# adaLN pieces of the second block in groups of four, all during the first block, in a two-block transformer on one core

## The chip, the core and the metric

The kernel runs on one core of one Trainium2 chip. The metric is the device time of one execution in microseconds (us), from the program's first to its last instruction; less is better. Inputs and weights lie in HBM, 582.56 MB of them are read once.

## The reference

256 latent tokens and 256 context tokens of width 1024, all in float32. A first block (adaLN, a mixer of bidirectional retention and mLSTM, a SwiGLU feed-forward) changes the latents; a second block of two layers follows. Each layer of the second block takes six vectors for shift, scale and gate from its own condition, once for the latents and once for the context:

```python
x = first_block(x, c, ctx, c_ctx, w_ada, ...)        # mixer, then x + g2 * swiglu(...)
for layer in range(2):                               # second block
    m_lat = split((silu(c_2) @ mod_w[layer] + mod_b[layer])[:, None, :], 6)
    m_ctx = split((silu(c_ctx_2) @ mod_w[layer] + mod_b[layer])[:, None, :], 6)
    h_lat = rms_norm(x_lat, norm1_g[layer]) * (1 + m_lat[1]) + m_lat[0]   # and h_ctx
    y = even_mixer(...) if layer == 0 else odd_mixer(...)   # window attention + gating; MLA + short conv
    x_lat = x_lat + m_lat[2] * y_lat
    h_lat = rms_norm(x_lat, norm2_g[layer]) * (1 + m_lat[4]) + m_lat[3]
    x_lat = x_lat + m_lat[5] * expert_choice_ffn(h_lat, ...)   # 16 experts, 32 tokens each
    # layer 0 does the same for the context
return rms_norm(x_lat, final_g)
```

`mod_w[layer]` is 1024 x 6144. It depends on the conditions alone, so these products can be made at any time before their layer.

## The kernel before

**The weight stream.** All weights come as pieces of up to 16 KB a partition (2 MB) in one order, written out with `seq(...)` (L220 to L227, L243). `Ring` (L48) puts the next piece of that order into whichever slot has just been used: `ring.done(slot)` issues its DMA on SP's queue (L69). Three slots, R0, R1 and R2, serve the dense stages; the expert stages have further ones (F, G, H, L, Y and others). A piece's slot is thus decided by which piece is used up first.

**The products.** `prod` (L331) splits a quarter of a piece at a time into a high and a low part (ACT at L303, then DVE at L304, into `w4k` or `w4p`) and makes three passes of 128x128 by 128x256 matmuls. Each job calls `tick()`, which takes one step of every generator in `beside`; `aside(...)` puts work there. In fin and fout, a piece `fin{i}` is 96 such matmuls, a pair of `fout` pieces 132.

**The adaLN pieces.** `moda0` to `moda11` are layer 0's, `modb0` to `modb11` layer 1's, 512 columns each. `mod_steps` (L354) is the generator of one: eight matmuls of 32 columns (`sT2`, the two conditions and zeros) against 512, four row groups side by side, into one of two `aux` PSUM banks; an evacuation to `ev`; four small matmuls with `selm` that turn `ev` into columns; an addition of the bias into MOD20 or MOD21. The profile counts two matmuls for each of these. In its rows the eight are `aux<-R,sT`, the four `aux<-cp,ev`.

**Stages in order.** Block 1's mixer ends with the product `wout`. A norm follows, then `fin0` to `fin10` and `fout0` to `fout7` (block 1's feed-forward), the even mixer (pieces `evkv`, `evin`, `evout`), the experts of layer 0, the odd mixer (`odq`, `odg`, ...) and the experts of layer 1. A scheduler decides each engine's order from the program.

**Where the pieces run before.** moda0 and moda1 after wout, moda2 and moda3 in fin, moda4 to moda6 in fout, moda7 to moda9 in the even mixer's attention, moda10, moda11 and modb0 to modb3 at its end, modb4 to modb11 in the odd mixer (`mods1`).

Of the kernel before, what the change touches and what calls it, by code (L numbers as in the profile page):

```python
# [14 lines left out]
P = 128  # L15
# [6 lines left out]
# pieces that come in parts, for the products that wait for them  # L22
# [6 lines left out]
class Rows:  # L29
    """An expert's piece with its four rows in more than one tile."""  # L30
# [17 lines left out]
class Ring:  # L48
    """Weight pieces in stream order through slots of 16 KB a partition."""
# [42 lines left out]
def body(ctx, tc, T, dbg=None, stop_at=None):  # L92
# [68 lines left out]
    # work in steps beside the products: each of their jobs takes a step of every generator  # L161
# [41 lines left out]
    # ---------------------------------------------------------------- weight stream  # L203
# [5 lines left out]
    def seq(*names):  # L209
# [12 lines left out]
        "wout0", "wout1", "moda0", "moda1")  # L222
# [20 lines left out]
    seq("odq0", "odg0", "modb4", "modb5", "odkv0", "oduq0", "odukv0",  "odg1", "modb6", "odg2", "modb7", "modb8",  # L243
        "modb9", "odout0", "odout1", "modb10", "modb11")
# [3 lines left out]
    # ---------------------------------------------------------------- constants and small loads  # L248
# [27 lines left out]
    selm = cp[:, 640:642]  # L276
    iota32 = cp[:, 642:674]
# [13 lines left out]
    # ---------------------------------------------------------------- shared parts  # L291
# [9 lines left out]
    def split(src, hi, lo):  # L301
        """src = hi + lo: hi keeps the bits of one pass, lo the rest."""
# [13 lines left out]
    def col(out, j, x, start=False):  # L316
        """A job of prod: 128 columns of the weights, from j * 128, as the partitions of out."""
# [6 lines left out]
    def tok(out, x, start=False):  # L324
        """A job of prod: tokens as the partitions of out, the weights' columns along it."""
# [5 lines left out]
    def prod(segments, jobs, quiet=False):  # L331
        """Each job's product over the rows of the weights' segments [128, k, n]; start: the first in its bank."""
# [21 lines left out]
    def mod_steps(name, sT, bias, MOD):  # L354
        """512 columns of both rows of silu(c) @ w + b, as columns of MOD[:, chunk, row], in steps."""
# [11 lines left out]
        ev = t2k() if name in ("modb10", "modb11") else work("ev", 512, 1)  # L367
# [3 lines left out]
        for c in range(4):  # L371
            mm(p2[:, 2 * c:2 * c + 2], ev[:, c * 128:c * 128 + 128], selm)
        dve.tensor_tensor(MOD[:, i * 4:i * 4 + 4, :], p2[:, :8].rearrange("p (c r) -> p c r", c=4),
                          bias[:, i * 4:i * 4 + 4, None].to_broadcast([P, 4, 2]), op=OP.add)

    def mod_steps0(name, sT, bias, MOD):
        """The same for the latents' row alone: weighted rows added up elementwise, then over the partitions."""
# [29 lines left out]
    def rstd_cols(ps, n, dim, half=False):  # L407
        """Columns [128, n] of 1 / sqrt(sum / dim + eps), halved if asked for, from sums."""
# [13 lines left out]
    def rms_bcast(chunks, ntok, dim):  # L422
        """1 / rms over the partitions and chunks of K-major [128, ntok] pieces, on every partition."""
# [11 lines left out]
    def norm_apply(X, rb, A, sh, hi, lo=None):  # L435
        """X * rstd * A + sh, K-major, 256 tokens: split into hi and lo, or whole in hi."""
# [38 lines left out]
    def sums_wide(bank):  # L475
        """The same with the tensor engine's sums, through a bank."""
# [33 lines left out]
    def rope(raw, sw, cosv, sinv, out, n, heads):  # L510
        """out = raw * cos + swap(raw) * sin; raw [128, heads * n] in SBUF."""
# [14 lines left out]
    # ================================================================ block 1  # L526
# [3 lines left out]
    sT2 = silu_c("cc2", cst.tile([P, KC * 32], F32, name="sT2"))  # L530
# [7 lines left out]
    def over_rms(X, read, U):  # L538
        """X / rms in U, before the scale and the shift are known."""
# [40 lines left out]
    # the first product starts with half of its rows  # L580
# [19 lines left out]
    # log of the decays, the same on every partition: columns (direction, head)  # L600
# [18 lines left out]
    # gates as rows: directions at partitions 0 and 32, the forget gates 64 further on  # L619
# [53 lines left out]
    # decays of the context's keys to its end (forward) and to its start (backward)  # L673
# [9 lines left out]
    # ---- projections  # L683
# [13 lines left out]
    def rope_pair(ps, scale, out):  # L697
        """Rotated heads of 128, two a bank: [128, 2, 256]."""
# [57 lines left out]
    def proj_T(name, post):  # L756
        """K-major [128, 256] products of the 512 columns, two a bank."""
# [16 lines left out]
    # ---- mLSTM and retention over the latent tokens  # L774
# [97 lines left out]
    def head_rstd(x, tag, dim):  # L872
        """Half of the rstd over each head's 128 of token-major [128, 512]."""
# [21 lines left out]
    # sigmoid(x) = (1 + tanh(x / 2)) / 2; the halves go into the factors beside it  # L895
# [1109 lines left out]
```

## Time and profile before

| | |
|---|---|
| median of three runs | 1931.47 us (1931.06 to 1933.48) |
| profiled execution, first to last instruction | 1936.9 us |
| mean granted TensorE clock | 0.939 |
| PE busy | 88% |
| weights and inputs read | 579.58 MB, 300 GB/s over the span |

The profile is of one execution, whose own time is its span. Where a view names an engine: PE is the tensor engine, DVE the vector engine, ACT the scalar engine, SP the engine whose queue issues nearly all DMAs. `R<-w_fin` is a DMA of a `fin` piece into a slot R.

### The profile page before, as it was taken

To read this page: it belongs to the slowest core of one execution; us is meant where nothing else is said; L and a number is where in the kernel's file an instruction comes from. 1 tells how busy PE (TensorE), PEld (TensorE's weight loads), DVE (VectorE), ACT (ScalarE), POOL (GpSimd) and SP (SyncE) were. 2 spreads that over 40 slices of the span, in tenths; PEclk is the share of its full clock that TensorE was granted. 3 is DMA by queue.
4 is the path that set the end of the run, shared out by engine and by line. 5 is a ranking of instruction groups with operands and counts; after the bars stand their busy time and mean duration, and the time that the engine had idled before them with its cause. 6 is when DMAs were issued, how large, how long until landed. Compare 5 with 4: busy or idle time off the path is not lost.

```text
span 1936.9 us, 29903 instructions
## 1 busy us (share of the span) xinstructions
PE 1696.5 (88%) x13020; PEld 1181.5 (61%) x13020; DVE 748.9 (39%) x1457; ACT 535.7 (28%) x927; POOL 52.1 (3%) x51
## 2 busy tenths in 40 slices
PE   7999999999999999799999989899999666575665
PEld 3999997989997678734433423368776323242333
DVE  4856785545566555502212102165653111010111
ACT  3323553445455543311010100043442100010000
POOL 0100020000001000000000000001000000000000
PEclk8999999999999999899999999999998988797877
DMA  9455456555633235699999999952687999999996
GB/s 354 183 199 218 158 192 228 195 226 182 251 129 111 113 141 216 261 408 425 428 428 427 427 428 427 423 207 109 239 326 306 425 426 426 425 425 426 426 427 261
DMA packets 53986, 582.56 MB, mean 301 GB/s; under 512 B 5984, under 2 KB 5984, under 8 KB 20576
## 3 DMA queue, kind: packets, MB, share of 16 engines
q1 hardware_dynamic: 53136, 577.90, 73.5%
q10 hardware_dynamic: 720, 2.75, 0.4%
q8 instruction: 102, 1.67, 0.3%
q14 instruction: 28, 0.23, 0.0%
HBM read 579.58 MB, written 1.05 MB: 300 GB/s over the span
## 4 chain that ended last, share of the span: by engine, by line
PE 56%; DMA 29%; issue 9%; DVE 4%; ACT 1%; POOL 0%; SPq 0%; DVEq 0%; ACTq 0%; POOLq 0%
PE acc L187 39%; PE aux L187 10%; DMA R<-w 8%; PE tr L187 5%; DMA H<-w 4%; DMA w4k<-w 3%; DMA F<-w 3%; DMA XC<-w 3%; DMA G<-w 2%; DMA L<-w 2%; PE tr L190 2%; DMA Y<-w 2%; PE lg L187 1%; DMA R<-w_in 1%; DMA cp<-cperm 1%
## 5 line engine op out<-in xcount | busy, mean ns | idle before, releaser
L187 PE MATMUL acc<-L,w4k 128*128 128x256 f32 (+3 forms) x1904 | 289.9, 343 | 17.1 <-DMA L<-w 14.0
L187 PE MATMUL acc<-H,w4k 128*128 128x256 f32 (+2 forms) x1608 | 245.8, 336 | 14.9 <-DMA H<-w 12.1
L187 PEld LDWEIGHTS acc<-L,w4k 128*128 128x128 f32 (+2 forms) x1904 | 218.5, 177 | 63.5 <-issue 33.1
L304 DVE TENSOR_TENSOR w4k<-R,w4k 128x1024 fp32r<-128x1024 f32 (+3 forms) x152 | 178.8, 1178 | 138.7 <-ACT w4k L303 137.1
L187 PEld LDWEIGHTS acc<-H,w4k 128*128 128x128 f32 (+2 forms) x1608 | 189.2, 176 | 54.6 <-issue 29.4
L303 ACT ACTIVATE w4k<-R 128x1024 fp32r<-128x1024 f32 (+3 forms) x152 | 154.3, 1017 | 223.1 <-PE acc L187 192.1
L187 PE MATMUL acc<-R,w4k 128*32 128x256 f32 (+1 forms) x1104 | 161.3, 549 | 58.2 <-DMA R<-w 58.2
L187 PEld LDWEIGHTS acc<-R,w4k 128*32 128x32 f32 (+1 forms) x1104 | 55.9, 139 | 147.5 <-DMA R<-w 71.7
L199 DVE COPY t2k<-acc 128x512 f32<-128x512 f32 x24 | 16.6, 691 | 283.3 <-PE acc L187 283.3
L187 PE MATMUL acc<-F,w4k 128*32 128x256 f32 (+2 forms) x624 | 89.1, 470 | 22.3 <-DMA F<-w 22.3
L197 ACT ACTIVATE w4p<-aux 32x512 f32<-32x512 f32 (+1 forms) x58 | 28.1, 485 | 256.3 <-PE aux L187 195.5
L187 PE MATMUL aux<-R,t2k 128*32 128x256 f32 (+2 forms) x592 | 84.2, 528 | 14.3 <-DMA R<-w 14.3
L199 DVE COPY w4p<-aux 32x512 f32<-32x512 f32 (+1 forms) x58 | 32.5, 560 | 144.4 <-ACT w4p L197 107.0
L187 PEld LDWEIGHTS acc<-F,w4k 128*32 128x32 f32 (+2 forms) x624 | 44.0, 144 | 56.3 <-DMA F<-w 26.7
L190 PEld LDWEIGHTS tr<-cp,t2k 128*128 128x128 f32 (+1 forms) x290 | 32.8, 146 | 72.9 <-ACT t2k L197 25.7
L197 ACT ACTIVATE t2k<-acc 128x512 f32<-128x512 f32 x24 | 14.3, 597 | 223.3 <-PE acc L187 223.3
L187 PE MATMUL acc<-G,w4k 128*128 128x256 f32 (+1 forms) x462 | 70.3, 333 | 6.2 <-DMA G<-w 6.2
L190 PE MATMUL tr<-cp,t2k 128*128 128x128 f32 (+1 forms) x290 | 47.6, 292 | 30.7 <-ACT t2k L197 12.1
L304 DVE TENSOR_TENSOR w4p<-R,w4p 128x1024 fp32r<-128x1024 f32 x43 | 53.1, 1235 | 41.2 <-ACT w4p L303 41.1
L187 PEld LDWEIGHTS aux<-R,t2k 128*32 128x32 f32 (+1 forms) x592 | 31.0, 138 | 59.3 <-issue 35.3
L187 PE MATMUL acc<-L,w4p 128*128 128x256 f32 x416 | 65.9, 281 | 0.0
L1265 DVE TENSOR_TENSOR t2k<-t2k,tr 128x256 f32<-128x256 f32 x16 | 6.7, 421 | 149.0 <-ACT t2k L1264 149.0
(465 smaller groups left out, 2635.6 us busy)
## 6 DMA issues: line engine op xcount, KB each, us to landing
R<-w SPq DMA_DIRECT2D x67, 2048.0 KB, 27.8
F<-w SPq DMA_DIRECT2D x23, 2048.0 KB, 29.4
H<-w SPq DMA_DIRECT2D x23, 2048.0 KB, 29.3
L<-w SPq DMA_DIRECT2D x23, 2048.0 KB, 26.2
Y<-w SPq DMA_DIRECT2D x23, 2048.0 KB, 28.5
R<-mod SPq DMA_DIRECT2D x22, 2048.0 KB, 8.8
R<-w_in SPq DMA_DIRECT2D x11, 2048.0 KB, 7.7
R<-w_fin SPq DMA_DIRECT2D x10, 2048.0 KB, 7.8
```

The source lines that it names most:

```text
L187: return pe.matmul(out, lhsT, rhs, start=start, stop=stop, **kw)
L190: return pe.transpose(out, in_, ident[:in_.shape[0], :in_.shape[0]])
L197: act.activation(out, in_, AF.Copy, scale=1.0 if scale is None else scale)
L199: dve.tensor_copy(out, in_)
L303: act.activation(rnd(hi), src, AF.Copy)
L304: dve.tensor_tensor(rnd(lo), src, hi, op=OP.subtract)
L1265: dve.tensor_tensor(hT[:, :256], sg[:, :256], pt[:, 256:], op=OP.mult)
```

## The change

The pieces run in groups of four. A group's four products go into one PSUM bank, each with a stationary shifted by two columns, so that they come to stand in rows of their own; one evacuation, four matmuls with an eight-column `selm` and one addition serve all four. All six groups are put beside the work after wout, as one chain. The stream alternates fin and mod pieces, then fout and mod pieces, and has no mod piece after evkv0. `need(name)` steps the chain until a piece has been issued. The comments and docstrings that the change also takes out are not shown.

```diff
+        "wout0", "moda0", "wout1", "moda1", "moda2")
+    mods = [f"moda{i}" for i in range(12)] + [f"modb{i}" for i in range(12)]
     for i in range(11):
-        seq(f"fin{i}", *{4: ['moda2'], 5: ['moda3']}.get(i, []))
-    seq("fout0", "fout1", "moda4", "fout2", "fout3", "moda5", "fout4", "fout5", "moda6", "fout6", "fout7")
-    seq("evkv0", "evin0", "evin1", "evin2", "moda7", "moda8", "moda9", "evout0", "evout1", "moda10", "moda11",
-        *[f"modb{i}" for i in range(4)])
+        seq(f"fin{i}", mods[3 + i])
+    for i in range(8):
+        seq(f"fout{i}", mods[14 + i])
+    seq("evkv0", *mods[22:], "evin0", "evin1", "evin2", "evout0", "evout1")
...
-    seq("odq0", "odg0", "modb4", "modb5", "odkv0", "oduq0", "odukv0",  "odg1", "modb6", "odg2", "modb7", "modb8",
-        "modb9", "odout0", "odout1", "modb10", "modb11")
+    seq("odq0", "odg0", "odkv0", "oduq0", "odukv0", "odg1", "odg2", "odout0", "odout1")
...
+    def mod_group(names, bias, MOD):
+        i0 = 4 * int(names[0][4:])
+        ps = None
+        for j, name in enumerate(names):
+            while not ring.has(name):
+                yield
+            s_, W = ring.get(name)
+            Wv = kv3(W)
+            ps = aux() if ps is None else ps
+            for k in range(2):
+                for q in range(4):
+                    mm(ps[32 * q:32 * q + 32, :], sT2[:, 2 * q + k, 6 - 2 * j:38 - 2 * j], Wv[:, 2 * q + k, :],
+                       start=j == 0 and k == 0, stop=j == 3 and k == 1, tile_position=(0, 32 * q), skip_group_check=True)
+            ring.done(s_)
+            yield
+        ev = work("ev", 512, 1)
+        evac(ev, ps)
+        yield
+        p2 = aux()
+        for c in range(4):
+            mm(p2[:, 8 * c:8 * c + 8], ev[:, c * 128:c * 128 + 128], selm)
+        dve.tensor_tensor(MOD[:, i0:i0 + 16, :].rearrange("p (i c) r -> p i c r", c=4),
...
+    def need(name):
+        while not ring.has(name):
+            tick()
+        return ring.get(name)
...
-    sT2 = silu_c("cc2", cst.tile([P, KC * 32], F32, name="sT2"))
+    sT2 = cst.tile([P, KC * 38], F32, name="sT2")
+    dve.memset(sT2, 0.0)
+    sT2 = sT2.rearrange("p (k m) -> p k m", k=KC)
+    act.activation(sT2[:, :, 6:8], S("cc2").rearrange("p (k m) -> p k m", k=KC), AF.Silu)
...
-    pre_ = aside(*[mod_steps(f"moda{i}", sT2, S("mod_b0"), MOD20) for i in [0, 1]])
+    groups_ = groups(*range(6))
...
-        s_, W = ring.get(f"fin{i}")
+        s_, W = need(f"fin{i}")
...
-        sa, Wa = ring.get(f"fout{2 * n4}")
-        sb, Wb = ring.get(f"fout{2 * n4 + 1}")
+        sa, Wa = need(f"fout{2 * n4}")
+        sb, Wb = need(f"fout{2 * n4 + 1}")
...
-    drain(mods_)
-    aside(*[mod_steps(f"moda{i}", sT2, S("mod_b0"), MOD20) for i in range(10, 12)],
-          *[mod_steps(f"modb{i}", sT2, S("mod_b1"), MOD21) for i in range(4)])
+    drain(groups_)
```

Every other `aside(mod_steps(...))` of moda and modb goes as well, and `mods1`.

**The boundary from wout to fin, on PE.** `acc<-H,w4p` is the end of wout, `tr<-ones` the norm's sums, `acc<-L,w4k` the first products of fin0. Before:

```order
L187 MATMUL acc_3324<-H_2829,w4p_3354 128x256
L187 MATMUL tr_3395<-ones,ss_3135 128x1
L187 MATMUL tr_3395<-ones,t2k_3383 128x1 x2
L187 MATMUL tr_3395<-ones,ss_3135 128x1
L187 MATMUL tr_3395<-ones,t2k_3383 128x1 x2
L187 MATMUL aux_3496<-cp,ev_3482 128x2 x4
L187 MATMUL aux_3502<-R_9_3131,sT_112 32x512 x8
L187 MATMUL tr_3406<-cp,rs_r_3404 128x128 x2
L187 MATMUL aux_3531<-cp,ev_3513 128x2 x4
```

Now:

```order
L187 MATMUL acc_3326<-H_2831,w4p_3356 128x256
L187 MATMUL aux_3450<-R_9_3133,sT_112 32x512
L187 MATMUL tr_3392<-ones,ss_3137 128x1
L187 MATMUL aux_3450<-R_9_3133,sT_112 32x512 x6
L187 MATMUL aux_3450<-R_10_3387,sT_112 32x512 x8
L187 MATMUL tr_3392<-ones,t2k_3385 128x1 x2
L187 MATMUL tr_3392<-ones,ss_3137 128x1
L187 MATMUL tr_3392<-ones,t2k_3385 128x1 x2
L187 MATMUL tr_3403<-cp,rs_r_3401 128x128 x2
L187 MATMUL acc_3464<-L_3391,w4k_3466 128x256
L187 MATMUL acc_3465<-L_3391,w4k_3466 128x256
L187 MATMUL aux_3450<-R_10_3490,sT_112 32x512 x8
```

moda1 (slot R_9) and moda2 (R_10) now stand among the norm's sums, where before the turn of moda0, moda1 and two more small turns stood behind them; no turn is there any more.

**The same place on SP's queue.** A cut piece comes in four DMAs (x4). Before, from wout1 on:

```order
L69 DMA R1_9_2848<-w_out 128x1024 x4
L69 DMA R2_9_3129<-mod0 128x4096
L69 DMA R0_9_3131<-mod0 128x4096
L69 DMA R2_10_3480<-w_fin 128x4096
L69 DMA R1_10_3385<-w_fin 128x1024 x4
L69 DMA R0_10_3511<-w_fin 128x4096
L69 DMA R1_11_3617<-w_fin 128x4096
```

Now, from moda0 on:

```order
L69 DMA R1_9_2850<-mod0 128x4096
L69 DMA R2_9_3128<-w_out 128x1024 x4
L69 DMA R0_9_3133<-mod0 128x4096
L69 DMA R1_10_3459<-w_fin 128x1024 x4
L69 DMA R2_10_3387<-mod0 128x4096
L69 DMA R0_10_3490<-mod0 128x4096
L69 DMA R2_11_3512<-w_fin 128x4096
```

fin0 (the cut `w_fin`) came into the slot of wout1 (R1_9), and comes now into that of moda0 (R1_9 of the second list); moda2 and moda3 are issued between it and fin1.

**fout, on SP's queue.** `mod0` and `mod1` are moda and modb pieces, the name left of the arrow is the slot with its number of use. Before, from the DMA of moda4 on:

```order
L69 DMA R1_15_4935<-mod0 128x4096
L69 DMA R2_15_5180<-w_fout 128x2816
L69 DMA R1_16_5030<-w_fout 128x2816
L69 DMA R0_15_5182<-mod0 128x4096
L69 DMA R1_17_5369<-w_fout 128x2816
L69 DMA R0_16_5219<-w_fout 128x2816
L69 DMA R2_16_5371<-mod0 128x4096
L69 DMA R0_17_5560<-w_fout 128x2816
L69 DMA R2_17_5410<-w_fout 128x2816
L69 DMA R1_18_5562<-ev_kv 128x2048
```

Now, from the DMA of modb5 on, to the one of ev_kv:

```order
L69 DMA R0_20_5320<-mod1 128x4096
L69 DMA R2_20_5472<-mod1 128x4096
L69 DMA R1_20_5474<-w_fout 128x2816
L69 DMA R0_21_5342<-w_fout 128x2816
L69 DMA R2_21_5512<-mod1 128x4096
L69 DMA R0_22_5672<-mod1 128x4096
L69 DMA R2_22_5534<-w_fout 128x2816
L69 DMA R1_21_5674<-w_fout 128x2816
L69 DMA R2_23_5865<-mod1 128x4096
L69 DMA R0_23_5713<-mod1 128x4096
L69 DMA R1_22_5867<-mod1 128x4096
L69 DMA R0_24_5735<-ev_kv 128x2048
```

Where two fout pieces came behind each other with a moda piece after them, each fout piece is now issued behind one or two modb pieces, and into the slots that these free: fout4 (R0_21) into that of modb5 (R0_20), ev_kv (R0_24) into that of modb9 (R0_23).

**The end of the odd mixer's attention, on PE.** `w4p,F` are attention's values, `E,F` its scores, `H,w4k` the products of odg. Before:

```order
L187 MATMUL acc_10905<-H_9970,w4k_10989 128x256
L187 MATMUL acc_10905<-H_9970,w4k_10990 128x256
L187 MATMUL aux_10933<-R_42_10672,sT_112 32x512 x8
L187 MATMUL aux_10959<-E_10021,F_10022 128x512
L187 MATMUL acc_11052<-w4p_10886,F_10022 64x128 x8
L190 MATMUL tr_11009<-cp,t2k_10873 128x128 x4
```

Now:

```order
L187 MATMUL acc_10857<-H_9960,w4k_10909 128x256
L187 MATMUL acc_10857<-H_9960,w4k_10910 128x256
L187 MATMUL aux_10898<-E_10011,F_10012 128x512
L187 MATMUL aux_10899<-E_10011,F_10012 128x512
L187 MATMUL acc_10953<-w4p_10838,F_10012 64x128 x8
L187 MATMUL acc_10971<-H_9960,w4k_10972 128x256 x2
```

The eight matmuls of the piece are gone from between the products and the scores; the rest keeps its order.

## Rows read from the trace of the kernel before

**Rows 1.** Page: PE's busy time; a split's DVE half (busy, mean ns | idle).

```profile
PE 1696.5 (88%) x13020; PEld 1181.5 (61%) x13020; DVE 748.9 (39%) x1457; ACT 535.7 (28%) x927; POOL 52.1 (3%) x51
...
L304 DVE TENSOR_TENSOR w4k<-R,w4k 128x1024 fp32r<-128x1024 f32 (+3 forms) x152 | 178.8, 1178 | 138.7 <-ACT w4k L303 137.1
```

**Rows 2.** Windows: length, PE, PEld, DVE, ACT, POOL, PEclk, DMA, GB/s.

```profile
350.00:550.00 200.00, 200.00 (x1644) 190.16 (x1643) 107.10 (x156) 93.32 (x133) 0.70 (x1) 0.99 0.58 215
...
620.00:700.00 80.00, 76.50 (x570) 57.71 (x570) 38.25 (x96) 46.78 (x86) 0.00 (x0) 1.00 0.28 108
...
850.00:1250.00 400.00, 369.68 (x1780) 146.59 (x1780) 71.39 (x131) 46.89 (x84) 0.14 (x2) 1.00 1.01 427
...
1500.00:1900.00 400.00, 252.39 (x2890) 123.66 (x2884) 39.73 (x90) 25.25 (x59) 0.00 (x0) 0.83 1.01 426
```

**Rows 3.** SP's DMA queue: first refills of the two expert stages (start, us).

```profile
820.76 3.76 SPq L69 DMA_DIRECT2D R<-w  x4
...
1482.87 2.06 SPq L69 DMA_DIRECT2D H<-w  x3
```

**Rows 4.** Chain, 415 to 500 us: start, us, what.

```profile
422.32 58.13 PE acc L187 x486
...
480.45 1.85 PE aux L187 x16
```

**Rows 5.** PE's timeline in both mixers: start, us, instruction.

```profile
622.91 0.95 PE L187 MATMUL aux<-cp,ev 128*128 128x2 f32 x8
...
623.79 1.92 PE L187 MATMUL aux<-R,sT 128*32 128x512 f32 x16
...
1427.96 1.96 PE L187 MATMUL aux<-sm,MOD 128*128 128x16 f32 x16
```

**Rows 6.** SP's DMA queue from wout to fin.

```profile
306.68 0.33 SPq L69 DMA_DIRECT2D R<-w_fin  x1
...
319.28 1.75 SPq L69 DMA_DIRECT2D R<-w_fin  x4
```

**Rows 7.** ACT's timeline at the same place.

```profile
324.59 1.06 ACT L303 ACTIVATE w4k<-R 128x1024 fp32r<-128x1024 f32 x1 [3.17 <-DMA R<-w_fin]
```

**Rows 8.** PE's timeline there: [idle before <-releaser].

```profile
328.77 0.61 PE L187 MATMUL tr<-ones,t2k 128*128 128x1 f32 x4 [3.10 <-ACT t2k L457]
...
332.08 3.64 PE L187 MATMUL aux<-R,sT 128*32 128x512 f32 x16
...
339.80 2.42 PE L187 MATMUL acc<-L,w4k 128*128 128x256 f32 x12 [1.31 <-DVE L L442]
```

**Rows 9.** DMA issues: count, KB, median us from issue to landing.

```profile
R<-mod SPq DMA_DIRECT2D x22, 2048.0 KB, 8.8
...
R<-w_fin SPq DMA_DIRECT2D x10, 2048.0 KB, 7.8
...
R<-w_fout SPq DMA_DIRECT2D x8, 1408.0 KB, 6.3
...
R<-ev_out SPq DMA_DIRECT2D x2, 2048.0 KB, 9.6
```

**Rows 10.** Pieces on PE: 340 to 576, 576 to 850, 1250 to 1490 us.

```profile
L187 PE MATMUL aux<-R,sT 128*32 128x512 f32 x80 | 11.7, 599 | 0.0
...
L187 PE MATMUL aux<-R,sT 128*32 128x512 f32 x144 | 17.4, 601 | 0.0
...
L187 PE MATMUL aux<-R,sT 128*32 128x512 f32 x96 | 14.8, 746 | 0.0
...
L187 PE MATMUL aux<-L,sT 128*32 128x512 f32 x32 | 3.8, 598 | 0.0
```

**Rows 11.** PE's timeline behind moda10 and behind modb11.

```profile
713.66 5.46 PE L187 MATMUL acc<-cph,G 128*128 128x128 f32 x24 [2.10 <-DVE G L1595]
...
1474.94 0.26 PE L190 MATMUL tr<-cp,t2k 16*128 16x16 f32 x2 [0.53 <-DVE t2k L1139]
```

**Rows 12.** Window of the clock at the boundary (columns as in Rows 2).

```profile
331.00:337.00 6.00, 6.00 (x28) 2.99 (x28) 0.95 (x3) 0.00 (x0) 0.03 (x1) 0.50 0.48 157
```

More of the change, by code (lines that the diff above doesn't have):

```diff
@@ L221, in body @@
         "win5", "ada8", "win6", "ada9", "win8", "win9", "win7", "win10", "ada10", "win11", "ada11", "up0", "up1",
-        "wout0", "wout1", "moda0", "moda1")
+        "wout0", "moda0", "wout1", "moda1", "moda2")
+    mods = [f"moda{i}" for i in range(12)] + [f"modb{i}" for i in range(12)]
     for i in range(11):
-        seq(f"fin{i}", *{4: ['moda2'], 5: ['moda3']}.get(i, []))
-    seq("fout0", "fout1", "moda4", "fout2", "fout3", "moda5", "fout4", "fout5", "moda6", "fout6", "fout7")
-    seq("evkv0", "evin0", "evin1", "evin2", "moda7", "moda8", "moda9", "evout0", "evout1", "moda10", "moda11",
-        *[f"modb{i}" for i in range(4)])
+        seq(f"fin{i}", mods[3 + i])
+    for i in range(8):
+        seq(f"fout{i}", mods[14 + i])
+    seq("evkv0", *mods[22:], "evin0", "evin1", "evin2", "evout0", "evout1")
     def expert_pieces(layer):
@@ L275, in body @@
     MB = cp[:, 512:640]
-    selm = cp[:, 640:642]
-    iota32 = cp[:, 642:674]
+    selm = cp[:, 640:648]
+    iota32 = cp[:, 648:680]
     ones = cst.tile([P, P], F32, name="ones")
@@ L366, in mod_steps @@
         ring.done(s_)
-        ev = t2k() if name in ("modb10", "modb11") else work("ev", 512, 1)
+        ev = work("ev", 512, 1)
         evac(ev, ps)
@@ L371, in mod_steps, with groups @@
         for c in range(4):
-            mm(p2[:, 2 * c:2 * c + 2], ev[:, c * 128:c * 128 + 128], selm)
+            mm(p2[:, 2 * c:2 * c + 2], ev[:, c * 128:c * 128 + 128], selm[:, 0:2])
         dve.tensor_tensor(MOD[:, i * 4:i * 4 + 4, :], p2[:, :8].rearrange("p (c r) -> p c r", c=4),
                           bias[:, i * 4:i * 4 + 4, None].to_broadcast([P, 4, 2]), op=OP.add)
+    def mod_group(names, bias, MOD):
[13 more added lines that the diff above has]
+            yield
+        ev = work("ev", 512, 1)
+        evac(ev, ps)
[4 more added lines that the diff above has]
+        dve.tensor_tensor(MOD[:, i0:i0 + 16, :].rearrange("p (i c) r -> p i c r", c=4),
+                          p2[:, :32].rearrange("p (c i r) -> p i c r", c=4, i=4),
+                          bias[:, i0:i0 + 16].rearrange("p (i c) -> p i c", c=4)[:, :, :, None].to_broadcast([P, 4, 4, 2]),
+                          op=OP.add)
+    def groups(*which):
+        return aside(*[mod_group([f"mod{'ab'[g // 3]}{g % 3 * 4 + j}" for j in range(4)],
+                                 S(f"mod_b{g // 3}"), (MOD20, MOD21)[g // 3]) for g in which])
+    def need(name):
+        while not ring.has(name):
+            tick()
+        return ring.get(name)
     def mod_steps0(name, sT, bias, MOD):
@@ L529, in body @@
     sT1 = silu_c("cc1", work("sT1", KC * 32, 1))
-    sT2 = silu_c("cc2", cst.tile([P, KC * 32], F32, name="sT2"))
+    sT2 = cst.tile([P, KC * 38], F32, name="sT2")
+    dve.memset(sT2, 0.0)
+    sT2 = sT2.rearrange("p (k m) -> p k m", k=KC)
+    act.activation(sT2[:, :, 6:8], S("cc2").rearrange("p (k m) -> p k m", k=KC), AF.Silu)
+    MOD20 = cst.tile([P, 48, 2], F32, name="MOD20")
+    MOD21 = cst.tile([P, 48, 2], F32, name="MOD21")
     MOD1 = cst.tile([P, 48, 2], F32, name="MOD1")
@@ L992, in body @@
     H2h, H2l = xv(H2), xv(H2[:, 2048:])
-    MOD20 = cst.tile([P, 48, 2], F32, name="MOD20")
-    MOD21 = cst.tile([P, 48, 2], F32, name="MOD21")
-    pre_ = aside(*[mod_steps(f"moda{i}", sT2, S("mod_b0"), MOD20) for i in [0, 1]])
+    groups_ = groups(*range(6))
     norm_sums(XLv, read, A2x, MOD1[:, 24:32, 0], H2h, H2l)
@@ L1021, in body @@
         ring.done(s_)
-        if i in (4, 5):
-            aside(mod_steps("moda%d" % {4: 2, 5: 3}[i], sT2, S("mod_b0"), MOD20))
-    drain()
     Ax0 = scale_vec("Ax0", MOD20, 1, 0, S("n1_0"))
@@ L1033, in body @@
     for n4 in range(4):
-        if n4 < 3:
-            aside(mod_steps(f"moda{4 + n4}", sT2, S("mod_b0"), MOD20))
-        sa, Wa = ring.get(f"fout{2 * n4}")
-        sb, Wb = ring.get(f"fout{2 * n4 + 1}")
+        sa, Wa = need(f"fout{2 * n4}")
+        sb, Wb = need(f"fout{2 * n4 + 1}")
         ps = acc()
@@ L1552, in window @@
                          lambda u: (S("sink")[:, u[0]:u[0] + 5:4], nsink[:, u[0]:u[0] + 5:4]), mask)
-    mods_ = aside(*[mod_steps(f"moda{i}", sT2, S("mod_b0"), MOD20) for i in range(7, 10)])
-    sk, Wk = ring.get("evkv0")
-    sq_, Wq = ring.get("evin0")
+    sk, Wk = need("evkv0")
+    sq_, Wq = need("evin0")
     keys_values(Wk, hc, N)
@@ L1730, in low_rank @@
             split(t, *outs(c))
-    def mods1(*rng):
-        return aside(*[mod_steps(f"modb{i}", sT2, S("mod_b1"), MOD21) for i in rng])
     s_, W = ring.get("odq0")
@@ L1745, in body @@
     low_rank([pa[:, :N], pa[:, N:], pb[:, :N]], N, 3, S("q_g"), 384, lambda c: (cqh[:, c, :], cql[:, c, :]))
-    m1 = mods1(4, 5)
     odg(0)
@@ L1829, in body @@
     ring.add("L")
-    m1 = mods1(6, 7, 8, 9)
     odg(1)
@@ L1851, in body @@
     finish()
-    mods1(10, 11)
     drain()
@@ L1903, in _constants @@
     ident = f32(p == f)
-    sel = f32([[q % 32 == j for j in range(2)] for q in range(P)])
+    sel = f32([[q % 32 == j for j in range(8)] for q in range(P)])
     iota = np.tile(np.arange(1, 33, dtype=np.float32), (P, 1))
```

## The prediction

> **What bounds the kernel now.** I read the page first: PE is busy 1696.5 of the profiled 1936.9 us [rows 1]. Such a mean mixes stages, so the next view is the table of windows. It shows two kinds of stage [rows 2]. From 350 to 550 us, which is block 1's FFN (fin, then fout), PE is busy in 200.00 of 200 us, at a clock of 0.99, while the DMA engines are busy 0.58: this stage lasts as long as PE's work. In the two expert stages the DMA engines are at 1.01 with 427 and 426 GB/s, and PE has holes; they last as long as their bytes. The mixers between (620 to 700 us is one piece of the even one) have PE busy in 76.50 of 80 us with DMA at 0.28: nearly PE-bound, but not quite, and the missing 4% is where an edit that takes PE work away may get less than it took.
>
> The timeline of SP's DMA queue says when an expert stage begins to refill its slots for the first time: 820.76 us and 1482.87 us [rows 3]. From there to its end a fixed number of pieces remains, at a saturated DMA. So an expert stage only shifts with its first refill, and what the change is worth is read in what happens before 820.76 and between the stages.
>
> **What one adaLN piece costs on PE.** The chain of the FFN stage, in which PE never pauses, gives 1.85 us for a piece's 16 recorded matmuls, and 58.13 us for 486 of the products' matmuls, that is 0.1196 us each [rows 4]. The four small ones that turn it start at 622.91 and the next row starts at 623.79: 0.88 us [rows 5]. I take 1.85 + 0.85 = 2.70 us a piece before. After, the turn is paid once for four pieces, with 8 columns instead of 2. No row has 8; the 16-column matmuls of the norm took 1.96 us for 16, 0.12 each or 0.98 for eight [rows 5], so a turn costs 0.85 to 0.98. I take 0.85 because a 2-column row is already no cheaper than 0.11 each. The shifted stationary is still 32 columns against 512, so 1.85 stays.
>
> **Boundary from wout to fin.** Before, fin0 goes into the slot that wout1 frees, at 319.28, and fin1 into the one that moda0 frees, at 306.68 [rows 6]. ACT then waits 3.17 us for fin0's first part [rows 7], its square for the norm is queued behind that split, PE waits 3.10 us for the square, and fin0's products run from 339.80 [rows 8]. After, the order of SP has fin0 in moda0's slot, so it is issued at about 307 and ACT's 3.17 us wait goes. On the other side moda2 (issued about 319) and moda3 (about 327, when moda1 is through) land 8.8 us later [rows 9], at 328 and 336. PE can do moda1 and moda2 among the norm's sums, and moda3 after two matmuls of fin0; fin0 gets going at about 337. Gain 3 us, with moda0 to moda3 done by then instead of moda0 and moda1.
>
> **The rest of fin and fout.** Before, five pieces ran there (80 recorded matmuls in the grouped rows, 16 a piece [rows 10]): 5 x 2.70 = 13.5 us. After, 20 pieces and six turns: 20 x 1.85 + 6 x 0.85 = 42.1 us. PE has no hole to hide them: +28.6 us, and this is the main cost of the change.
>
> **New waits for DMA.** The ring has three slots, and each now alternates between a weight piece and a mod piece. A fin takes 96 x 0.1196 = 11.5 us, a pair of fouts 132 x 0.1196 = 15.8 us. I walked the stream of SP with these, the landing times 7.8 (fin), 8.8 (mod) and 6.3 us (fout) [rows 9], and 2.2 us for the split of a piece's first quarter into two parts (1.06 on ACT [rows 7], then 1.18 on DVE [rows 1]). Nearly every piece lands 1 to 4 us ahead of its use. Two don't. fout4 stands behind modb5 in slot R0: it is issued at about 520 and is wanted split at about 526, so PE waits some 3.7 us. ev_kv stands behind modb9 in R0, which PE takes only at the end of fout: some 1.8 us. Together 5.5 us, from 3 (if the pieces before them come a little early) to 11 (if all land 2.2 us later). I take 5.5, the walk with the medians. So the even mixer begins 28.6 + 5.5 - 3 = 31 us later.
>
> **What the mixers give back.** The even mixer loses nine pieces (144 recorded matmuls [rows 10]): 9 x 2.70 = 24.3 us. One of them, moda10, lies ahead of a matmul that then still waits 2.10 us for DVE [rows 11]; taking it away only lengthens that wait, so 2.7 don't come back. In the order the context's gathers move to the end of the latents' products, which I estimate at 1 us lost. Back: about 21 us. The odd mixer loses eight (96 in slot R and 32 in L [rows 10]): 8 x 2.70 = 21.6 us at the full clock. modb11 lies inside the wait for the top-k: behind it PE had to wait only 0.53 us more for DVE [rows 11], so about 2.1 of it stays as waiting. Back: 19.5 us. The rows' own sum there, 14.8 + 3.8, is above 8 x 1.92 because two of them ran at the half clock, which I don't count as a gain.
>
> **Expert stages.** Same bytes, same slots, DMA saturated: 0. Vector work: 18 evacuations and adds fewer, on engines that wait for PE in these stages: 0. The longer wait for moda and modb values costs nothing, since all are there before the even mixer.
>
> **Sum.** 31 - 21 - 19.5 = -9.5 us on the profiled execution of 1936.9, whose span is 0.28% above the median of the runs, 1931.47. I subtract it from the median: about **1922 us**.
>
> **Clock.** After the 3.10 us wait at the boundary PE ran at 0.50 from 331 to 337 us [rows 12], one of the two levels, 1.2 GHz; a piece's 16 matmuls took 3.64 us there against 1.92 [rows 5, 8]. So a wait of such a length cost some 3 us more behind it. The Trainium skill, "TensorE: Matmul & The Clock Gate", section "HAM oscillation — how this bites in real kernels", says that a wait for DMA between groups of matmuls lets the clock fall, so that the next group starts at half rate each time. By that rule the trace agrees at this place, and it speaks against a change that puts DMA waits into a stage that had none. By it the two waits would cost about 6 us more and the sum would be -3.5; by the rows of a stage without a wait, nothing more. I stay with the second, since the change also takes away the boundary's wait and its slow 6 us, which I did not count as a gain either.
>
> **Rivals.**
> *Cover comes back.* The mixers' 24.3 and 21.6 us fall only partly, because attention's softmax chains and norms, which the pieces filled, now show as waits. For: PE had only 3.5 us of holes in 620 to 700 with two pieces in it, so something was filled. Against: most pieces stand between long runs of products. If a quarter more is lost, 10 us: 1932.
> *The clock falls at the new waits.* One or both: 3 to 6 us, **1925 to 1928**.
> *No waits, all visible.* fout4 and ev_kv come in time (5.5), and the mixers return all but 2 us of 45.9 (3.4): about 1913. For: these two are the only late pieces of the walk, and both hang on when PE takes the mod piece before them.
> *The ring is too thin (slower).* Three slots must turn over two pieces in each fin. The margin in the walk is about 2.6 us over the 7.7 us it takes on the mean, and about 15 pieces follow one another through the slots. Landing times up to 9.6 us (ev_out, 2 MB) stand in the trace [rows 9]. From 10.3 us on, each microsecond costs 15; the change breaks even at 10.9, and at 11.3 it ends at about 1937. For: two pieces of 2 MB in 13.4 us are 313 GB/s, and 215 GB/s took 0.58, so DMA comes to about 0.84. Against: that is still under the 1.01 of the expert stages, where transfers queue.
> That the pieces aren't moved is excluded: the order has all of them before the even mixer.
>
> **How the numbers follow.** My forecast 0.50 (1916 to 1927), the clock 0.14, cover back 0.13, the thin ring 0.11, all visible 0.12. A measurement of this kernel tells 0.2%, 3.9 us, from no change: below 1927.6 is faster, above 1935.3 slower. My forecast, all visible, and about two thirds of the clock case are faster, with a little of the cover case: 0.74. The rest of the clock case and most of the cover case: 0.15. The thin ring: 0.11. Range: from 1911, all visible with a little margin, to 1932, the cover case; the thin ring is left out.
>
> **What would show it.** All aux matmuls of the pieces end before the even mixer, with six turns. fin0's products start near 337. PE waits 3 to 4 us for R<-w_fout before the third pair and about 2 for R<-ev_kv, and nowhere in fin. The even mixer's first product comes 31 us later; the first refill of the first expert stage near 831 instead of 820.76; from there to the second stage's first refill 19.5 us less. Wrong would be: waits for R<-w_fin or R<-mod at each fin (thin ring), a clock below 0.9 in 340 to 580 us, or a mixer that shrinks by under 16 us.

## The result, and the profile after

The changed kernel takes 1915.16 us (median of four runs, 1914.26 to 1917.97) against 1932.47 for the kernel before in the same measurement: a ratio of 0.991, 95% interval 0.9894 to 0.9925. Beside the experiments below it took 1918.85 us, ratio 0.9928 (0.9909 to 0.9948). So it is faster by some 13 to 17 us; 9.5 were forecast.

To see where they come from, I cut both spans at five places that every kernel here has: the first of the norm's sums behind wout, the start of the last run of fout's products out of H, SP's first refill of the first expert stage, the DMA of od_q, and the first gather of the second expert stage. The table of windows of the kernel before, cut there (length, PE, PEld, DVE, ACT, POOL, PEclk, DMA, GB/s; in order fin and fout, the even mixer, the first experts, the odd mixer, the last stage):

```profile
325.39:547.28 221.89, 217.09 (x1743) 203.79 (x1742) 120.93 (x182) 101.47 (x147) 1.41 (x2) 0.97 0.56 207
547.28:820.76 273.48, 256.00 (x1957) 215.13 (x1957) 153.20 (x347) 125.64 (x233) 13.44 (x12) 0.95 0.42 160
820.76:1252.44 431.68, 401.36 (x1928) 157.73 (x1926) 73.22 (x135) 49.17 (x88) 0.14 (x2) 1.00 1.00 423
1252.44:1476.37 223.93, 209.71 (x1520) 164.10 (x1517) 126.02 (x253) 92.09 (x166) 8.41 (x7) 0.95 0.61 233
1476.37:1936.90 460.53, 300.09 (x3498) 155.50 (x3497) 52.10 (x120) 34.06 (x79) 3.16 (x4) 0.83 0.96 403
```

The same of the changed kernel:

```profile
323.14:570.29 247.15, 239.09 (x1947) 204.90 (x1946) 118.24 (x181) 98.78 (x144) 1.41 (x2) 0.97 0.78 307
570.29:819.84 249.55, 232.71 (x1797) 200.50 (x1797) 145.30 (x331) 121.00 (x227) 13.11 (x12) 0.96 0.32 122
819.84:1250.65 430.81, 401.13 (x1928) 159.11 (x1926) 73.21 (x135) 49.27 (x88) 0.14 (x2) 1.00 1.00 424
1250.65:1457.65 207.00, 186.43 (x1337) 152.18 (x1333) 122.34 (x242) 90.21 (x162) 8.57 (x7) 0.95 0.46 178
1457.65:1913.00 455.35, 292.77 (x3488) 154.09 (x3488) 51.71 (x118) 34.07 (x79) 3.16 (x4) 0.84 0.96 404
```

Block 1 is 25.3 us longer, the even mixer 23.9 shorter although the last three pieces and their turn now run in its first microseconds, the first experts the same, the odd mixer 16.9 shorter, and the last stage 5.2 shorter. The first refill comes at 819.84 us, 0.9 earlier than in [rows 3]; the prediction had it 10 later. Ahead of the first cut the changed kernel is 2.2 shorter. These two executions lie 23.9 us apart, more than the medians do; a second trace of each kernel, below, has 14.3. So what one pair of traces has of a few microseconds in one stage can be chance.

The waits of PE in block 1 of the changed kernel (what it waited for: us in total, times, longest):

```profile
PE acc L187 <- ACT w4p L303: 3.3, 1, 3.3
PE aux L187 <- DMA R<-mod: 2.2, 1, 2.2
PE acc L187 <- ACT L L480: 1.1, 1, 1.1
PE tr L187 <- POOL rs_r L452: 1.0, 1, 1.0
```

The first is fout4, whose split waits for the transfer behind modb5: the timeline has 3.28 us of idle before its first product at 533.91 (3.46 in the second trace), where the prediction had 3.7. The second is moda3. PE's timeline at the boundary, which answers to [rows 8]:

```profile
331.15 0.50 PE L187 MATMUL acc<-L,w4k 128*128 128x256 f32 x2 [1.11 <-ACT L L480]
333.82 3.64 PE L187 MATMUL aux<-R,sT 128*32 128x512 f32 x16 [2.17 <-DMA R<-mod]
337.39 6.53 PE L187 MATMUL acc<-L,w4k 128*128 128x256 f32 x46
```

fin0 begins at 331.15, moda3's eight matmuls stand in the queue behind its first two, and the rest of fin0 runs from 337.39. The windows of the two waits, which answer to [rows 12]:

```profile
331.00:337.00 6.00, 3.68 (x18) 0.89 (x18) 5.07 (x13) 2.61 (x7) 0.00 (x0) 0.62 1.01 429
...
520.00:530.00 10.00, 10.00 (x85) 7.42 (x88) 1.58 (x3) 0.27 (x1) 0.00 (x0) 1.00 1.00 422
530.00:540.00 10.00, 6.26 (x32) 5.33 (x25) 4.73 (x7) 3.89 (x6) 0.00 (x0) 0.69 0.84 297
```

Before the wait for fout4 the granted clock was 1.00, in the ten microseconds with it 0.69. In the second trace of the changed kernel it was 0.86 from 530 to 540 us and 0.96 from 540 to 550. The pieces themselves, by shape, between 300 and 600 us:

```profile
L187 PE MATMUL aux<-R,sT 128*32 128x512 f32 x376 | 49.7, 618 | 2.2 <-DMA R<-mod 2.2
L187 PE MATMUL aux<-cp,ev 128*128 128x8 f32 x48 | 6.0, 248 | 0.0
```

48 small matmuls are six turns, at 248 ns each like the 2-column ones.

### The profile page after: what moved, and what is told of

The parts are those of the page before. It is cut to its first block, busy times and chain, and to the rows that moved or that the text cites. A ratio compares the mean times of both kernels' runs of the same rounds, so it can differ in the third digit from the quotient of the medians.

```text
span 1913.0 us, 29571 instructions
## 1 busy us (share of the span) xinstructions
PE 1662.7 (87%) x12876; PEld 1153.6 (60%) x12876; DVE 738.2 (39%) x1430; ACT 529.0 (28%) x916; POOL 52.7 (3%) x51
## 5 line engine op out<-in xcount | busy, mean ns | idle before, releaser
L187 PE MATMUL acc<-L,w4k 128*128 128x256 f32 (+3 forms) x1744 | 269.3, 328 | 12.6 <-DMA L<-w 9.5
L187 PEld LDWEIGHTS acc<-L,w4k 128*128 128x128 f32 (+2 forms) x1744 | 207.1, 178 | 53.0 <-issue 32.4
L187 PE MATMUL acc<-R,w4k 128*32 128x256 f32 (+1 forms) x1136 | 157.4, 513 | 45.6 <-DMA R<-w 45.6
L187 PE MATMUL aux<-R,t2k 128*32 128x256 f32 (+3 forms) x656 | 87.8, 512 | 20.7 <-DMA R<-w 20.3
L187 PE MATMUL acc<-G,w4k 128*32 128x256 f32 (+1 forms) x622 | 87.5, 408 | 20.6 <-DMA G<-w 20.6
L187 PE MATMUL acc<-F,w4k 128*32 128x256 f32 (+2 forms) x464 | 74.5, 450 | 8.3 <-DMA F<-w 8.3
L187 PEld LDWEIGHTS acc<-G,w4k 128*32 128x32 f32 (+1 forms) x622 | 57.8, 166 | 37.6 <-DMA G<-w 26.4
L197 ACT ACTIVATE t2k<-acc 128x512 f32<-128x512 f32 x24 | 14.3, 597 | 217.3 <-PE acc L187 217.3
L187 PE MATMUL acc<-Y,w4k 128*32 128x256 f32 (+1 forms) x464 | 56.7, 477 | 16.5 <-DMA Y<-w 16.5
L303 ACT ACTIVATE w4p<-R 128x1024 fp32r<-128x1024 f32 x43 | 45.6, 1060 | 75.3 <-PE acc L187 61.2
```

The lines of the kernel that those rows point to most:

```text
L187: return pe.matmul(out, lhsT, rhs, start=start, stop=stop, **kw)
L197: act.activation(out, in_, AF.Copy, scale=1.0 if scale is None else scale)
L303: act.activation(rnd(hi), src, AF.Copy)
```

## The experiments

Lengths of the five stages in the traces, cut as above (us; the profiled execution of each kernel, which can lie some microseconds off its median; each ratio is to the kernel before as measured beside that run; five more kernels are told in the text):

| kernel | fin, fout | even mixer | experts | odd mixer | last stage | median of runs | ratio to before, 95% |
|---|---|---|---|---|---|---|---|
| before | 221.9 | 273.5 | 431.7 | 223.9 | 460.5 | 1932.47 | |
| before_again | 221.6 | 272.8 | 431.9 | 223.5 | 460.5 | 1935.4 (one) | |
| changed | 247.2 | 249.6 | 430.8 | 207.0 | 455.4 | 1915.16 | 0.9894 to 0.9925 |
| after_again | 247.2 | 251.4 | 430.6 | 206.9 | 458.6 | 1918.85 | 0.9909 to 0.9948 |
| no_mixer_mods | 221.8 | 241.2 | 432.8 | 207.0 | 456.5 | 1884.28 | 0.9733 to 0.9774 |
| mixer_no_turn | 220.4 | 275.6 | 432.7 | 225.6 | 458.6 | 1935.4 | 1.0007 to 1.0034 |
| group_only | 211.6 | 273.9 | 431.5 | 224.6 | 457.4 | 1930.84 | 0.9976 to 1.0007 |
| group_block1 | 210.2 | 279.4 | 432.1 | 225.7 | 456.5 | 1927.69 | 0.998 to 1.0002 |
| b_stay | 228.3 | 241.6 | 432.4 | 218.1 | 458.4 | 1905.73 | 0.9849 to 0.9878 |

**A second trace of before (before_again).** Unchanged kernel.

> The kernel before, once more, for a second trace of it. Theory A (the first trace of before holds a chance excess of some 5 us: its span was 1936.9 us where the runs had a median of 1931.47, and TensorE was at the half clock in stretches without a wait, in 480 to 490 and 760 to 790 us, and in the tail after the last weights): the span is about 1930, those two stretches are at the full clock, the tail after 1900 us is at a clock near 0.85, and the even mixer from the end of fout to the first refill of the experts takes 3 to 5 us less than 270.2. Theory B (the excess belongs to the kernel, the adaLN pieces in the mixers cause it): the same stretches are slow again and that distance is 270 us.

The span was 1933.6 us, and every stage came within 1 us of the first trace. The stretch at 480 to 490 us was at the full clock this time, the one at 770 to 780 was low again, at 0.83, and the last 20 us again at 0.76. So most of what looked like chance repeats: theory B for the even mixer and the tail. In these two traces the five stages agree to 1 us, but the two of the changed kernel differ by 1.8 us in the even mixer and 3.3 in the last stage. So a difference of under some 3 us between two rows of the table shows nothing by itself.

**The mixers without their pieces (no_mixer_mods).** Seventeen pieces are left out of stream and program:

```diff
-    seq("evkv0", "evin0", "evin1", "evin2", "moda7", "moda8", "moda9", "evout0", "evout1", "moda10", "moda11",
-        *[f"modb{i}" for i in range(4)])
+    seq("evkv0", "evin0", "evin1", "evin2", "evout0", "evout1")
...
+    seq("odq0", "odg0", "odkv0", "oduq0", "odukv0", "odg1", "odg2", "odout0", "odout1")
...
-    mods_ = aside(...)    and the other asides of moda7 to moda11 and modb0 to modb11
```

> The kernel before without moda7 to moda11 and modb0 to modb11: they are neither loaded nor computed, and their columns of the modulation are zero. This is what the mixers have to give back, with nothing put into block 1. Theory A (a piece costs its 2.70 us of PE, and one or two lie in waits): 17 x 2.70 less 5 is 41 us, about 1891 us. Theory B (a piece in a mixer costs more than its own PE time, since it also delays attention and the clock falls): 48 us or more, 1884 us or below.

1884.28 us, 47.5 less: theory B's number. The even mixer went from 273 to 241.2 us, the odd one from 223.7 to 207.0:

```profile
545.35:786.58 241.23, 226.81 (x1741) 200.72 (x1741) 145.85 (x328) 120.70 (x227) 13.42 (x12) 0.95 0.27 104
...
1219.42:1426.41 206.99, 185.70 (x1336) 152.67 (x1333) 121.48 (x240) 90.23 (x162) 8.58 (x7) 0.95 0.46 178
```

The mean granted clock is 0.95 in both mixers with the pieces and without, so a lower clock is not what these traces show as the reason. The changed kernel has 249.6 and 207.0 there, and three late pieces and a turn, 3 x 1.92 + 1.06 = 6.8 us, are in the first: it got nearly all that there was to get.

**The even mixer alone without its nine (no_even_mods).** The first line of that diff and its asides only.

> The kernel before without the nine pieces of the even mixer (moda7 to moda11, modb0 to modb3; not loaded, not computed, their columns of the modulation are zero); the eight of the odd mixer stay. Theory A (from the traces, 273 us against 241 in the even mixer): 32 us less, about 1900 us, and so the two mixers are not alike: 3.5 us a piece here against 2 in the odd one. Theory B (the sum of the prediction, 21 us): 1911 us.

1901.15 us against 1928.56 of before, measured beside it, ratio 0.9861 (0.9845 to 0.9878), 27 us; by the trace the even mixer was 241.1 us long again, 32 less. Theory A, or near it: nine pieces of 2.70 us, 24.3 of PE, take 27 to 32 out of the stage, and the prediction's 21 was too low. The eight of the odd mixer are then worth 17 us by the traces, and 20 by the runs (47.5 less 27.4).

**The move without the groups (move_only).**

```diff
-        return aside(*[mod_group([f"mod{'ab'[g // 3]}{g % 3 * 4 + j}" for j in range(4)], ...) for g in which])
+        return aside(*[mod_steps(f"mod{'ab'[g // 3]}{g % 3 * 4 + j}", sT2[:, :, 6:38], ...)
+                       for g in which for j in range(4)])
```

> The changed kernel's stream and places, but each piece alone in its bank, with its own evacuation, its own four small matmuls and its own addition (24 turns instead of 6). Theory A (a turn is 0.85 us of PE where PE is the bound): 18 x 0.85 is 15 us more than the changed kernel, about 1930 us, that is no gain over before by the move alone. Rival (the turns fill waits or run beside other work): within 5 us of the changed kernel, 1920 us or below, and the move alone is worth 12 us.

1937.59 us, ratio 1.0036 (1.0021 to 1.0052): the move alone makes the kernel slower. Theory A had the direction and 15 us; it was 19 to 22 us over the changed kernel, so a turn costs 1.0 to 1.2 us here (over 18 turns) and not 0.85. From the end of wout to the end of fout it took 269.1 us against 247.2.

**The groups without the move (group_only).**

```diff
-    pre_ = aside(*[mod_steps(f"moda{i}", sT2, S("mod_b0"), MOD20) for i in [0, 1]])
+    pre_ = aside(group("a", 0, 1, 2, 3))
...
+        if n4 == 0:
+            aside(group("a", 4, 5, 6))
...
+    mods_ = aside(group("a", 7, 8, 9))
...
+    aside(group("a", 10, 11), group("b", 0, 1, 2, 3))
```

> The kernel before with its stream and its places, but neighbouring pieces in groups that share a bank and a turn: a0 to a3, a4 to a6, a7 to a9, a10 and a11, b0 to b3, b4 and b5, b6 to b9, b10 and b11 (8 turns instead of 24). Theory A: 16 x 0.85 is 13.6 us, some 2 of it in waits, so about 11.5 us less than before, about 1921 us. Rival (in the mixers the turns fill waits): only the 4 to 5 us of block 1, about 1928 us.

1930.84 us, ratio 0.9991: nothing that can be measured. By its trace block 1 is 10 us shorter, and neither mixer is shorter, with 11 turns less in them. The profiled execution took 1924.68 us, 6 below the median, in which the 10 us do not show.

**The turns left out of the mixers (mixer_no_turn).** This is the other side of the same question:

```diff
         ring.done(s_)
+        if name.startswith("modb") or name in [f"moda{j}" for j in range(7, 12)]:
+            return
-        ev = t2k() if name in ("modb10", "modb11") else work("ev", 512, 1)
+        ev = work("ev", 512, 1)
...
```

> The kernel before; the 17 pieces of the two mixers (moda7 to moda11, modb0 to modb11) are loaded and multiplied, but their evacuations, small matmuls and additions are left out, and their columns of the modulation stay zero. Theory A (a turn in a mixer is on the path of PE like the eight matmuls): 17 x 0.88 = 15 us, about 1917 us. Theory B (turns and evacuations there only fill waits, as grouping them in place brought nothing): within 4 us of before, 1928 us or more; then the 47 us that the mixers gave back when the pieces were left out come from the eight matmuls, and from what their DMAs and places do to attention.

1935.4 us, ratio 1.0021: theory B, and no gain at all from 15 us less of PE's work. PE's waits in its even mixer:

```profile
PE tr L190 <- DVE t2k L1143: 5.9, 1, 5.9
PE aux L187 <- ACT pp L1440: 5.3, 2, 4.3
PE acc L187 <- DVE G L1599: 3.8, 1, 3.8
PE aux L187 <- DMA R<-mod: 3.7, 1, 3.7
```

In the first trace of the kernel before:

```profile
PE acc L187 <- DVE G L1595: 2.1, 1, 2.1
PE aux L187 <- ACT pp L1436: 1.8, 2, 1.0
PE tr L190 <- DVE pp L1451: 1.3, 1, 1.3
PE tr L190 <- ACT G L1452: 1.3, 1, 1.3
```

The wait for a mod piece was not there in the first trace of before, and 0.7 us in the second. The pieces of the attention follow one another through one slot; with less to do between them PE comes to the next before it has landed, waits 3.7 us in its queue with attention behind it, and the softmax comes late after that. group_only shows the same wait, 3.9 us. In the odd mixer there is no such wait for a piece: PE's busy time fell there by 7.3 us and its idle time rose from 14.2 to 23.1, so there the turns only filled waits.

**The groups in block 1 alone (group_block1).** As group_only, with the mixers' pieces single.

> The kernel before; only the seven pieces that it has in block 1 are grouped (a0 to a3, a4 to a6), the other 17 run singly in the mixers as before. Theory A (a turn costs more than its 0.88 us where PE is the bound, above all at the boundary from wout to fin, where two ran at the half clock; the trace with all grouped in place had 10 us less from the end of wout to the end of fout): 10 us less than before, about 1922 us. Theory B (a turn costs 0.85 us and no more): 5 turns less, 4 us, about 1928 us.

1927.69 us, ratio 0.9991 (0.998 to 1.0002). Neither theory: block 1 was 11 us shorter in the trace, as theory A said, but the even mixer 6 us longer, with the pieces there unchanged. PE waited 3.5 us there for `w4p` and 2.2 for `ev`, both from DVE. Other waits went or shrank, so PE's idle time is 18.7 us there against 17.5: the waits make only 1.2 of the 6. The rest is busy time, at a mean granted clock of 0.94 against 0.95, and its cause is open. The profiled execution took 1930.58 us, 3 above the median.

**The odd mixer's pieces stay (b_stay).**

```diff
+    mods = ([f"moda{i}" for i in range(12)] + [f"modb{i}" for i in range(12)])[:16]
...
-        seq(f"fout{i}", mods[14 + i])
+    for i, n in enumerate([0, 1, 0, 1, 0, 0, 0, 0]):   # mod pieces after fout{i}
...
     seq("odq0", "odg0", "modb4", "modb5", ...)   as before, with its asides
```

> The changed kernel, but modb4 to modb11 stay in the odd mixer as in the kernel before; 16 pieces in four groups are moved, with two mod pieces in fout. Theory A (from the two traces: the odd mixer's eight pieces gave back 16.7 us there and cost 8 x 1.85 + 2 x 0.9 = 16.6 in block 1, and the wait of 3.3 us for fout4 with the slow clock behind it goes): 5 us less than the changed kernel, about 1910 us. Rival (the last expert stage took 5 us less after the change because the slots are free earlier at the end of the odd mixer, which is lost again): 1915 us.

1905.73 us, ratio 0.9864: 9 to 13 us faster than the changed kernel, more than theory A had. By the traces eight pieces fewer make block 1 and the head of the even mixer 27 us shorter (18.9 and 8.0), and the odd mixer only 11 longer. Of the 27, 15 are the pieces' matmuls, 2 two turns, 4 the waits for fout4 and its split, 3 the slow clock behind them; 3 are left without a name. The odd mixer is 218.1 us here with the same eight pieces that it has in the kernel before, where it is 223.7; the mean granted clock is 0.97 here and 0.95 there, and why is open.

**modb10 and modb11 stay (b1011_stay).**

> The changed kernel, but modb10 and modb11 alone stay at the end of the odd mixer, as in the kernel before (22 pieces moved). Theory A (they are free there: in the changed kernel PE waits 5.9 us for the top-k, and in the kernel before the last piece's matmuls lay in that wait): block 1 is 2 x 1.85 us shorter and the odd mixer not longer, about 1911 us. Rival (they hold a slot until the top-k is through, so the last expert stage gets its weights later): 1916 us or more.

1922.25 us, ratio 0.9945 (0.993 to 0.9961): not faster. The odd mixer took only 2.7 us more than the changed one's, so the two are nearly free there as theory A had it, but block 1 was not shorter: fout4's wait was still there (3.2), and at the head of the even mixer PE waited another 3.2 us for ev_kv's split, now without modb11's matmuls ahead of it. The rival's reason is wrong too, since the last stage was 457.2 us, within what unchanged kernels differ by.

**No fout piece behind a late mod piece (no_fout_wait).**

```diff
-        seq(f"fout{i}", mods[14 + i])
+    for i, n in enumerate([1, 1, 0, 1, 0, 1, 0, 1]):   # mod pieces after fout{i}
```

> The changed kernel with all 24 pieces moved, but five mod pieces instead of eight among the fout pieces, so that fout4 and ev_kv stand behind no mod piece that is used late; the last five pieces follow ev_kv. Nothing else differs. Theory A (a wait for DMA costs itself and about as much again at the half clock behind it: 3.3 + 0.8 of waits and 3.1 of clock in the trace): 7 us less than the changed kernel, 1910 us (its two medians were 1915.2 and 1918.9). Theory B (a wait costs itself alone): 4 us less, 1913 us. Rival (the five pieces at the head of the even mixer cost there what they saved, or wait for DMA): 1917 us or more.

1922.37 us, ratio 0.994: the rival. fin and fout were 12.6 us shorter. Two pieces and one turn fewer ran in that stage, which are 5.8 by the rows; the other 7 are 4 us less of PE's idle time and about 3 of busy time, theory A's wait and its clock (1.00 in every ten microseconds from 500 to 560 us). But the last pieces now came close behind each other, with 15 to 17 of ev_kv's products, some 2 us, between them, and the even mixer took 266.4 us, 16.8 more. This is what PE waited for at its head (565 to 605 us):

```profile
PE aux L187 <- DMA R<-mod: 4.0, 2, 2.9
PE acc L187 <- ACT w4k L306: 3.4, 1, 3.4
PE aux L187 <- DVE ev L199: 0.8, 1, 0.8
```

**The best version (b_stay_mended).** b_stay with moda3 behind fin1 in the stream (`[0] + [1] * 10` mod pieces after the fins, one after fout1, fout3 and fout5).

> The kernel with modb4 to modb11 left in the odd mixer (1905.7 us), and moda3 behind fin1 in the stream instead of ahead of it, so that PE does not wait for it before fin0's products. Theory A (in that trace PE waited 1.7 us for moda3 and was at the half clock for some 7 us behind it, which is 3.5 us more): 3 to 5 us less, about 1902 us. Rival (moda3 then comes late inside fin0 instead, and the norm's chain sets the half clock there anyway): 1905 to 1907 us.

1902.88 us, ratio 0.9842 (0.9818 to 0.9867). Its timeline at the boundary:

```profile
331.12 0.65 PE L187 MATMUL acc<-L,w4k 128*128 128x256 f32 x2 [1.11 <-ACT L L484]
332.93 8.03 PE L187 MATMUL acc<-L,w4k 128*128 128x256 f32 x46 [1.16 <-DVE L L485]
...
341.24 1.92 PE L187 MATMUL aux<-R,sT 128*32 128x512 f32 x16
```

No wait for moda3, which runs at 341.24 at the full clock. This is the fastest kernel here that leaves nothing out, by its median, but the step from b_stay isn't shown by the times: 2.9 us lie between the medians, and the two intervals (0.9849 to 0.9878 and 0.9818 to 0.9867) overlap. Fin and fout were 1.1 us shorter in the trace. The 46 products took 8.03 us where they took 6.53 in the changed kernel, so most of what moda3's wait and its slow matmuls had cost is spent there, at the lower clock behind the norm's waits.

**The changed kernel again (after_again).**

> The changed kernel once more, beside the others of this call: 1915 us, and a second trace. If the tail behind the last weights is at a clock of 0.8 again (it was 0.75 in both traces of before), the 3 to 4 us there belong to the kernel; if it is at 0.75, they are chance.

1918.85 us. The tail was at 0.84 in the last 20 us (0.76 in both traces of before), but it was between 0.65 and 0.84 in the other kernels, and the last stage between 455.4 and 460.5, with its pieces untouched. I leave those 2 to 5 us open.

## Why the prediction was right, and where its sum was off

The direction and the range held, and so did the mechanism in fin and fout. The sum was 4 to 8 us too small: one term, the even mixer, was much too low, and others, the boundary and by the traces the odd mixer, were too high and made up for part of it. That they partly cancel is luck. The gain lies between the forecast and the rival "no waits, all visible" (about 18 us). Of that rival the mixers' half was true: they gave back 47.5 together, where it had 43.9. Of its two waits ev_kv's nearly went and fout4's stayed.

- **Boundary.** Right in what happens, not in its worth. fin0 was issued early, its first products came at 331.15, and ACT's wait went. But from the first of the norm's sums to the steady products it took 14.2 us against 14.4, in both pairs of traces, where a gain of 3 was forecast: moda3's wait and its matmuls at the half clock took the rest. The 2.4 us between 337.39 and the 339.80 of [rows 8] are an earlier start of the whole stage, which the second traces have the other way round (338.80 and 337.68).
- **The rest of fin and fout.** Right: 17 pieces and five turns up to the end of fout less 13.5, with 3.7 of waiting, are +25.9 by the steps of the prediction, and from fin0's steady products to that end the traces have 232.9 us against 207.5, +25.4 (+25.9 in the second pair). The mean clock of that stretch is 0.98 before and after (0.99 and 0.98 in the second pair): the kernel before has nearly as much half clock there, at other places, so the sum held without a term for it. The three late pieces, with turn and wait, were 8.2 by the steps and 8.1 in the trace (249.6 against the 241.4 of a mixer without pieces; 10.0 in the second trace).
- **The new waits.** fout4's was at its place with 3.3 for 3.7. ev_kv's was 0.35 for 1.8 here, and 3.2 in the kernel where modb10 and modb11 stayed. moda3's 2.2 was in the forecast only as fin0's start near 337, not as a wait of PE in fin.
- **The even mixer: the step that failed.** "Back: about 21 us" was 32 by the trace, 27 by the runs. Three things make the difference. The rows of the nine pieces are 17.4 us for their products [rows 10] and 8.6 for their turns, so 26.0 and not 24.3. PE's busy time fell by 29 in the kernel without pieces, 3 more than the rows, and why is open. And taking pieces away did not lengthen the other waits on the whole, for which, with the gathers, the prediction took off 3.7: the wait of 2.10 us behind moda10 [rows 11] grew to 4.3, but four waits of attention, 4.4 us together, went, and in the kernel without pieces PE's idle time fell by 3. The first row is the turns in the kernel before, the second that wait in the changed one:

```profile
L187 PE MATMUL aux<-cp,ev 128*128 128x2 f32 x72 | 8.6, 242 | 0.7 <-ACT ev L197 0.7
...
PE acc L187 <- DVE G L1631: 4.3, 1, 4.3
```

- **A price by row.** The turns' rows did not tell what leaving them out is worth: with turns, with fewer turns or with none, the even mixer stayed at 273 to 279 us as long as the nine pieces came through its slots. Whether the eight matmuls, the transfers or their places in PE's queue cost the 27 to 32 us was not tried apart. Each kernel here is also scheduled anew, so that a stage can differ by more than the edit.
- **The odd mixer.** 16.8 by the traces for 19.5, 20 by the runs, so at most a little less than forecast. The rival "cover comes back" shows in the waits: PE's idle time rose from 14.2 to 20.6 us, and the wait for the top-k, 0.53 behind modb11 [rows 11], is 5.9 now. Since the same eight cost 27 us in block 1 and at the head of the even mixer, moving them was a loss, which b_stay shows. The wait in the changed kernel:

```profile
PE tr L190 <- DVE t2k L1176: 5.9, 1, 5.9
```

- **Expert stages.** The first was 0.9 us shorter, as good as the 0 forecast. The last was 2 to 5 shorter, unexplained.
- **A turn.** 0.85 was too low where turns were added: move_only makes it 1.0 to 1.2, and group_block1's five turns fewer came with 11 us less in block 1. In the mixers it is 0. The gain of the change needs both halves: the move alone loses 6 us, the groups alone bring none, both together 13 to 17.
- **Clock.** The wait for fout4 was 3.3 us, and the clock over those ten microseconds 0.69, which is 3.1 us more; in the second trace it is some 1.8 more. no_fout_wait got about 7 us back in that stretch when that wait was gone. So this rival's mechanism was real, at one of its two places. The rule of the Trainium skill that the prediction named ("TensorE: Matmul & The Clock Gate", section "HAM oscillation — how this bites in real kernels": a wait for DMA lets the clock fall) agrees with this row.
- **The thin ring.** Landing times went up from 7.8 to 9.6 us for fin and from 6.3 to 7.1 for fout (medians), not enough to stop fin. It is the pieces close behind each other at the head of the even mixer, in no_fout_wait, that three slots were too few for.

## What to carry to other kernels

What a small job beside an in-order engine's queue costs is not its busy time: leave it out, or leave its half out, and see how the stage moves; here the same job cost 3.0 to 3.5 us in one stage, 2.1 to 2.5 in another, and its second half nothing in both. Work that costs less where it stands than where it would go (the odd mixer's pieces) should stay there; work that costs its stage more than its own time (the even mixer's) is worth moving even into a stage that is full. When pieces for side work share a small ring with the main stream, a main piece should not stand behind a side piece that is used late, and side pieces need enough products between them: 11.5 us of a fin were enough here, 2 us were not.

## What was not expected of the hardware

A wait for DMA in a stage that is otherwise full cost more than itself: 3.3 us of waiting ahead of 533.91 us and 3.1 us at the lower clock of 1.2 GHz in one trace, 3.5 and some 1.8 in the other. Stretches of the half clock also came without a wait in front: 0.86 in 480 to 490 us in the first trace of before and 1.00 there in the second, 0.87 and 0.83 in 770 to 780 in the two, with PE busy in all of these. Why is open.
